# Early norms of the token parts, a refill of x inside the last pair, and first Down operands made ahead

## The chip, the cores and the metric

The kernel runs on one core of one Trainium2 chip, in one launch. The metric is the device time in microseconds, the median of the runs. Engines are named as in the profile: PE is TensorE, DVE VectorE, ACT ScalarE, POOL GpSimd, SP the engine that issues transfers.

## The reference

One step of a two-layer trunk in float32, for 1024 prompt frames and 32 sample frames, model width 1024. Layer 0 is retention and a ConvFFN, layer 1 is GLA (gated linear attention) and a ConvFFN.

```
h = rmsnorm(x, g)                      # per frame
q, k, v, g = split(h @ w_in)           # layer 0: 4 heads, q, k 256 wide, v, g 512
q, k = rotary(q, pos), rotary(k, pos)
S, o = chunked recurrence (q, k, v)    # S: 256 x 512 per head, decay per head
x = x + (silu(g) * groupnorm(o)) @ w_out
u = rmsnorm(x) @ w_up; c = 3-tap causal conv of u
x = x + (silu(gate) * val) @ w_down    # width 2816
```

All states and the last two rows of u are outputs too, and the frames end in a final RMSNorm.

## The kernel before

Frames stand in the columns and features in the 128 partitions: x is 8 tiles (kt) by 1056 columns, which are cut in four chunks of 264 (TH columns, 256 prompt and 8 sample frames each). A product of float32 accuracy is made of three matmuls: each operand is split in a rounded head and the rest (XA holds both for x, `whi` and `wlo` for a weight), and head by head, head by rest and rest by head are added in a PSUM bank. A weight tile is loaded to a `raw` tile by SP, ScalarE casts its head and VectorE subtracts.

Layer 0 starts in `ret_in`. Its first stage, the prelude, handles the four chunks one after the other. `normal(c)` squares x on ScalarE (L663), adds the squares on GpSimd for chunks 1 to 3 (L665), sums over partitions by matmuls with ones into `pn` (L671), makes 1/rms by a logarithm and an exponential on ScalarE and three operations on VectorE (the row, L673 and L166 to L168), and then `pair` scales x (L651, two tiles), casts the head (L654, ScalarE) and subtracts (L655, VectorE). `plain(j, c)` makes q or k of head 0 from it by 48 matmuls (L687 to L689, into `pj`); L690 copies them out. `sums(s)` adds chunks 2s and 2s+1 for the next stage.

That stage makes the gates of all heads and q, k of heads 1 to 3 with 14 units, two token halves and seven products each, a fast block product in which sums of blocks replace an eighth of the multiplications (`seven`, matmuls L351 to L356 into `pu`, 12 to a product). `put` adds products into a room of the buffer ARi (L718). What a product needs of the first feature half of an odd chunk is overwritten by sums, so that at the end of `ret_in` these parts are made again from x: the refill (L772 to L777), for each half one transfer, four multiplies, cast and subtraction.

Retention runs over four heads and nine steps (m) in each, eight for 128 prompt frames and one for the sample. The scores `pss` are masked (L492, `pm`), v is made into `psv` from weights wlo/wx, the outputs go to `po`, the state to `pu`, and the normalised output is `on` (L593).

`second(l)` then runs `Down` with w_ro (layer 0) or w_go (layer 1), the up projection with the convolution, `Down` with w_down, and for layer 0 the GLA. Down walks over column chunks; in each it goes through the weight tiles (kt), and for each through eight output columns (nt), each with a bank `pd` of its own. `load` fetches a tile's weight and its rows of the activation and splits both (XH, XB, hh, hl). When a column has its last tile, `evict` adds the bank to the residual (L1332, L1392). After the last chunk of layer 0's second Down the GLA's projections `pj` (L122) start.

Each engine runs its instructions in order, and the order is the program's, unless `order(a, b)` forces one; buffers come from pools with a fixed number of tiles, and from rooms cut by hand out of ARi. The order below is that of the built program.

## Time and profile before

| | |
|---|---|
| Median of 3 runs | 2955.16 us (2955.0 to 2959.51) |
| Profiled execution | 2953.43 us, span 2951.6 |
| TensorE busy | 2838.1 us (96%), 20658 matmuls |
| VectorE, ScalarE, GpSimd busy | 67%, 45%, 11% |
| Mean rate of transfers | 119 GB/s over the span |

The page divides the span in 40 slices of 74 us; TensorE's busy share is 0.4 in the first slice, 0.8 or more in all others, and the granted clock 0.7 in the first and 0.9 or more after it. A matmul record has a start and a modelled end, so that neighbours overlap; the step from start to start is what one costs. Times of the rows below are counted from the start of the span.

### The profile page before, as it was taken

How to read it: one execution, taken by the hardware profiler on the slowest of the kernel's cores; microseconds unless marked ns; L12 is line 12 of the kernel's file. 1: busy time of each engine (PE TensorE's matmuls, PEld its weight loads, DVE VectorE, ACT ScalarE, POOL GpSimd, SP SyncE). 2: the span in 40 equal slices, each digit the busy share in tenths (PEclk: the TensorE clock that was granted, in tenths of full speed). 3: DMA queues.
4: the chain of work that ended last, by engine and by line, in shares of the span. 5: the costliest groups of instructions: out<-in, count | busy, mean ns of one | idle time of the engine just before them, and what ended most of it. 6: DMA issues, size and time to landing. Idle time of an engine off the chain costs nothing.

```text
span 2951.6 us, 51990 instructions
## 1 busy us (share of the span) xinstructions
PE 2838.1 (96%) x20658; PEld 2732.8 (93%) x20658; DVE 1986.3 (67%) x3298; ACT 1325.7 (45%) x2375; POOL 335.7 (11%) x565
## 2 busy tenths in 40 slices
PE   4899989999899999999999999999998999999998
PEld 4899977878799999999999989999998999999998
DVE  6667546666578887777654577775488777786544
ACT  3332554343455444444543455554254444444443
POOL 1112000000002011111000032220011111110000
PEclk7999999999999999999999999999999999999999
DMA  3133343342576322222665511113652222227554
GB/s 118 37 95 117 110 151 101 94 127 82 176 250 191 112 73 80 80 74 82 218 198 172 185 43 47 47 40 130 202 173 74 86 80 73 87 69 239 179 162 142
DMA packets 206739, 353.83 MB, mean 120 GB/s; under 512 B 35712, under 2 KB 146432, under 8 KB 206496
## 3 DMA queue, kind: packets, MB, share of 16 engines
q1 hardware_dynamic: 205952, 349.93, 36.8%
q8 instruction: 161, 2.64, 0.4%
q14 instruction: 82, 0.67, 0.1%
q10 hardware_dynamic: 544, 0.59, 0.1%
HBM read 271.50 MB, written 78.95 MB: 119 GB/s over the span
## 4 chain that ended last, share of the span: by engine, by line
PE 85%; DVE 7%; DMA 3%; ACT 2%; issue 1%; POOL 1%; DVEq 0%; SPq 0%; ACTq 0%; POOLq 0%
PE pu L356 13%; PE pu L351 13%; PE pu L355 13%; PE pd L1171 7%; PE pd L1173 7%; PE pd L1172 7%; PE psv L245 2%; PE psv L244 2%; PE psv L246 2%; DMA raw<-w_ro 2%; PE pg L122 1%; PE pg L123 1%; PE pg L124 1%; PE pl L899 1%; PE pj L122 1%
## 5 line engine op out<-in xcount | busy, mean ns | idle before, releaser
L102 DVE TENSOR_TENSOR wlo<-raw,whi 128x1024 fp32r<-128x1024 f32 x226 | 283.7, 1257 | 259.4 <-ACT whi L102 250.3
L102 ACT CAST whi<-raw 128x1024 fp32r<-128x1024 f32 x226 | 236.4, 1049 | 313.2 <-PE pd L1172 219.5
L1171 PE MATMUL pd<-hh,whi 128*128 128x384 f32 (+1 forms) x880 | 284.9, 324 | 0.0
L1172 PE MATMUL pd<-hl,whi 128*128 128x384 f32 (+1 forms) x880 | 284.2, 323 | 0.1
L1173 PE MATMUL pd<-hh,wlo 128*128 128x384 f32 (+1 forms) x880 | 283.8, 323 | 0.0
L334 ACT COPY HR<-pu 128x264 f32<-128x264 f32 x264 | 99.0, 375 | 314.0 <-PE pu L356 311.5
L356 PE MATMUL pu<-XA,wgl 128*128 128x264 f32 x752 | 213.7, 284 | 0.7 <-DVE wgl L314 0.7
L355 PE MATMUL pu<-XA,wgh 128*128 128x264 f32 x752 | 212.9, 283 | 0.0
L351 PE MATMUL pu<-XA,wgh 128*128 128x264 f32 x752 | 212.8, 283 | 0.0
L1171 PE MATMUL pd<-XH,whi 128*128 128x264 f32 x576 | 164.2, 289 | 10.4 <-ACT XH L1146 7.6
L1172 PE MATMUL pd<-XH,whi 128*128 128x264 f32 x576 | 164.5, 287 | 2.7 <-DVE XH L1147 2.6
L1172 PEld LDWEIGHTS pd<-hl,whi 128*128 128x128 f32 x880 | 165.2, 188 | 0.9 <-DVE hl L1147 0.4
L1171 PEld LDWEIGHTS pd<-hh,whi 128*128 128x128 f32 x880 | 165.2, 188 | 0.4
L1173 PEld LDWEIGHTS pd<-hh,wlo 128*128 128x128 f32 x880 | 165.2, 188 | 0.1
L1239 DVE SCALAR_TENSOR_TENSOR AR<-AR,cw 128x1058 f32<-128x1058 f32 x88 | 116.0, 1318 | 72.1 <-ACT AR L1238 72.1
L1173 PE MATMUL pd<-XH,wlo 128*128 128x264 f32 x576 | 162.5, 287 | 0.7 <-DVE wlo L102 0.7
L314 DVE TENSOR_TENSOR wtl<-rv,wth 128x1024 fp32r<-128x1024 f32 x58 | 71.8, 1237 | 120.7 <-ACT wth L313 119.4
L1219 DVE TENSOR_TENSOR AR<-HR,pu 128x264 f32<-128x264 f32 (+2 forms) x440 | 144.7, 368 | 4.6 <-PE pu L356 4.6
L356 PEld LDWEIGHTS pu<-XA,wgl 128*128 128x128 f32 x752 | 141.2, 188 | 1.0 <-DVE wgl L314 1.0
L351 PEld LDWEIGHTS pu<-XA,wgh 128*128 128x128 f32 x752 | 141.3, 188 | 0.2 <-ACT wgh L313 0.2
L355 PEld LDWEIGHTS pu<-XA,wgh 128*128 128x128 f32 x752 | 141.2, 188 | 0.0
L351 PE MATMUL pu<-XA,wsh 128*128 128x264 f32 x464 | 132.0, 284 | 4.6 <-DVE ARi L718 2.5
(433 smaller groups left out, 9669.7 us busy)
## 6 DMA issues: line engine op xcount, KB each, us to landing
raw<-w_down SPq DMA_DIRECT2D x120, 512.0 KB, 3.6
raw<-w_ro SPq DMA_DIRECT2D x55, 512.0 KB, 4.4
rg<-w_up SPq DMA_DIRECT2D x44, 512.0 KB, 3.5
rv<-w_up SPq DMA_DIRECT2D x44, 512.0 KB, 3.5
scr_h<-AR SPq DMA_DIRECT2D x44, 512.0 KB, 2.7
HR<-scr_h SPq DMA_DIRECT2D x84, 192.0 KB, 3.7
raw<-w_go SPq DMA_DIRECT2D x23, 512.0 KB, 4.1
HR<-scr_or SPq DMA_DIRECT2D x64, 132.0 KB, 4.4
```

Of the source, the lines that this page charges most:

```text
L102: ins = S.copy(hi, raw), V.tensor_tensor(lo, raw, hi.bitcast(F32), op=ALU.subtract)
L122: PE.matmul(ps, hi[:, k], rh, start=kt == 0, stop=False)
L314: V.tensor_tensor(l_, src, h.bitcast(F32), op=ALU.subtract)
L334: S.copy(t, b)
L351: mm = PE.matmul(ps, wh[:, k], x[:, 0, kt], start=m in (1, 2, 4, 5) and kt == 0, stop=False, skip_group_check=True)
L355: PE.matmul(ps, wh[:, k], x[:, 1, kt], start=False, stop=False, skip_group_check=True)
L356: mm = PE.matmul(ps, wl[:, k], x[:, 0, kt], start=False, stop=kt == 3, skip_group_check=True)
L1171: PE.matmul(o, w[0][:, k], h[0][:, :n], start=i == 0, stop=False)
L1172: PE.matmul(o, w[0][:, k], h[1][:, :n], start=False, stop=False)
L1173: self.last_mm = PE.matmul(o, w[1][:, k], h[0][:, :n], start=False, stop=i == nk - 1)
L1219: V.tensor_tensor(u[:, d:d + n], t[:, o:o + n], b[:, o:o + n], op=op)
L1239: V.scalar_tensor_tensor(cj, uj[:, 1:T + 3], cw[:, nt, 1:2], cj, op0=ALU.mult, op1=ALU.add)
```

## The change

Five edits.

1. In `ret_in` the loads of chunk 0 stand first and its four squares ahead of the weight casts. Chunks 1 to 3 are squared with four tiles at a time, and the squares have a place of their own (`spare`), so that they need no tile of the weights' pool; chunk 0's x stands in `spare` too, and chunk 3 no longer waits for chunk 0's room. GpSimd adds 1056 and then 528 columns per chunk in place of 792 and 528, and two matmuls do instead of three. The row of chunk k+1 is placed within the k-th product. Each chunk's q and k are made one after the other. The second half of XC is allocated after `spare` is closed.
2. The rotations of head 0's q and k are placed between the products of the second token half, in units 1 to 4, with the room `ts` of ARi as their temporary. The second half starts after 8.5 products of the first instead of 7.3.
3. `refill` is called within the last unit, for each half as soon as its last product that needs the old values is issued. The first takes the room `ts`, the second `u`. The copies of the sample columns go to head 0, m = 2.
4. Both first Down objects are made before retention. In the last head's turn, `early` loads and splits weight tiles 0 and 1 and their rows for chunk 0.
5. In layer 0's second Down, last column chunk, the eight residual adds are issued first, and splits, squares and stores after the last of them.

```diff
+                if m == 4 and h + 1 == RH:
+                    d1s[0].early(0)
+                    d1s[0].early(1)
+                if m == 2 and h == 0:
+
+                    for j in range(4):
+                        for f in range(2):
+                            S.copy(xs[:, 4 * f:4 * f + 4, j * TS:j * TS + TS].rearrange("p k (c t) -> p k c t", c=4),
+                                   XP[:, :, f, j // 3, :, TH - 8:TH].rearrange("p c k t -> p k c t").bitcast(F32))
...
-        room = rooms(u=(AR, [8 * TH, 0, 4 * TH], 4 * TH), sn=ring(12 * TH, TH, 6, AR), ts=ring(18 * TH, 4 * TH, 1, AR))
...
+        room = rooms(u=(AR, [0, 8 * TH, 12 * TH], 4 * TH), sn=(AR, [o * TH for o in (4, 5, 6, 7, 16, 17)], TH),
+                     ts=ring(18 * TH, 4 * TH, 1, AR))
...
-        def normal(c):
-            per = 2 if c == 0 else 3
-            sq = []
+        def squares(c):
+            per = 2 if c == 0 else 4
+            sq = spare[:, (8 + c % 2 * 8) * TH:(16 + c % 2 * 8) * TH].rearrange("p (k t) -> p k t", k=KT)
             for kt in range(0, KT, per):
-                n = min(per, KT - kt)
-                t = w_tile(f"sq{uid()}").bitcast(F32)[:, :n * TH].rearrange("p (k t) -> p k t", k=n)
-                S.activation(t, xr[c][:, kt:kt + n], AF.Square)
-                if c and kt:
-                    G.tensor_tensor(sq[0][:, :n], sq[0][:, :n], t, op=ALU.add)
-                else:
-                    sq.append(t)
-            sq = [t[:, k] for t in sq for k in range(per)]
+                ins = S.activation(sq[:, kt:kt + per], xr[c][:, kt:kt + per], AF.Square)
+            n = KT
+            while c and n > 2:
+                n //= 2
+                G.tensor_tensor(sq[:, :n], sq[:, :n], sq[:, n:2 * n], op=ALU.add)
+            return sq, n, ins
+
+        def row(c, sq, n, after):
             ps = sm("pn")[:, :TH]
-            for i, t in enumerate(sq):
-                PE.matmul(ps, ones, t, start=i == 0, stop=i == len(sq) - 1)
-            t = w_tile(f"rm{uid()}").bitcast(F32)
-            V.tensor_scalar(t[:, :TH], ps, 1.0 / D, EPS, op0=ALU.mult, op1=ALU.add)
-            rsqrt(R[:, c * TH:c * TH + TH], t[:, TH:2 * TH], t[:, :TH])
+            for i in range(n):
+                mm = PE.matmul(ps, ones, sq[:, i], start=i == 0, stop=i == n - 1)
+                if after is not None:
+                    order(mm, after)
+            V.tensor_scalar(sq[:, 0], ps, 1.0 / D, EPS, op0=ALU.mult, op1=ALU.add)
+            rsqrt(R[:, c * TH:c * TH + TH], sq[:, 1], sq[:, 0])
+
+        def parts(c):
...
+        def refill(s):
+            c = 2 * s + 1
+            a = room("u" if s else "ts").rearrange("p (k t) -> p k t", k=4)
+            nc.sync.dma_start(a, io["xP"][:, c, 0:4])
+            for k in range(4):
+                V.scalar_tensor_tensor(a[:, k], a[:, k], gcol[:, 0, k:k + 1], R[:, c * TH:c * TH + TH],
+                                       op0=ALU.mult, op1=ALU.mult)
+            S.copy(XP[:, c, 0, 0], a)
+            V.tensor_tensor(XP[:, c, 0, 1], a, XP[:, c, 0, 0].bitcast(F32), op=ALU.subtract)
...
-        normal(0)
-        plain(0, 0)
-        normal(1)
-        plain(0, 1)
-        normal(2)
-        plain(0, 2)
-        plain(1, 0)
-        plain(1, 1)
-        sums(0)
-        for kt in range(0, KT, 4):
-            nc.sync.dma_start(xr[3][:, kt:kt + 4], io["xP"][:, 3, kt:kt + 4])
-        normal(3)
-        plain(0, 3)
-        plain(1, 2)
-        plain(1, 3)
-        sums(1)
-        weight_sums(0)
+        sq, n, ins = squares(0)
+        for j in range(2):
+            w0[j] = load_w(io["w_rqk"][0, j], None, (ins, None))
+        fetch(1, 4)
+        w0[2] = load_w(io["w_rqk"][0, 2])
+        row(0, sq, n, None)
+        fetch(2, 4)
+        fetch(3, 4)
+        w0[3] = load_w(io["w_rqk"][0, 3])
+        ones_ident()
+        cos = const("cos", [P, T], pl=rk)
+        sin = const("sin", [P, T], pl=rk)
+        gn = const("rgn", [P, 16], pl=rk)
+        parts(0)
         for c in range(4):
             for j in range(2):
-                ts = raw_tile(f"ts{uid()}")[:, :2 * TH].rearrange("p (j t) -> p j t", j=2)
-                rotate(qk0[c][:, j], ts, c, TH)
+                k = 2 * c + j
+                if k < 3:
+                    sq, n, _ = squares(k + 1)
+                mm = plain(j, c)
+                if k < 3:
+                    row(k + 1, sq, n, mm)
+            if c < 3:
+                parts(c + 1)
+            if c == 1:
+                sums(0)
+        first.close()
+        more(1, es.enter_context(pool("xd", side="right")).tile([P, 24 * TH], F32R, tag="XD", name="XD"))
+        weight_sums(0)
+        sums(1)
+        turns = [(c, j) for c in range(4) for j in range(2)]
         n = 7 * len(units)
-        seq = [(k, 0, k) for k in range(n)] + [(max(k + 3.5, 7.3 + 0.6 * k), 1, k) for k in range(n)]
+        seq = [(k, 0, k) for k in range(n)] + [(max(k + 3.5, 8.5 + 0.6 * k), 1, k) for k in range(n)]
...
-        for s in range(2):
-            c = 2 * s + 1
-            a = room("u").rearrange("p (k t) -> p k t", k=4)
-            nc.sync.dma_start(a, io["xP"][:, c, 0:4])
-            for k in range(4):
-                V.scalar_tensor_tensor(a[:, k], a[:, k], gcol[:, 0, k:k + 1], R[:, c * TH:c * TH + TH],
-                                       op0=ALU.mult, op1=ALU.mult)
-            S.copy(XP[:, c, 0, 0], a)
-            V.tensor_tensor(XP[:, c, 0, 1], a, XP[:, c, 0, 0].bitcast(F32), op=ALU.subtract)
+            if s == 1 and i in (2, 5) and f and turns:
+                c, j = turns.pop(0)
+                ts = room("ts")[:, :2 * TH].rearrange("p (j t) -> p j t", j=2)
+                rotate(qk0[c][:, j], ts, c, TH)
+            if f == len(units) - 1 and ORD[i] == 5:
+                refill(s)
...
+        held = []
         with pool("db") as dp:
             def evict(c, nt, a, ps, ss):
                 c0, n = CM[c]
                 V.tensor_tensor(a, a, ps, op=ALU.add)
-                split_x(2, a, nt, c0, n)
-                sumsq(ss, nt, a, n)
-                nc.sync.dma_start(scr_x[:, nt, c0:c0 + n], a)
+
+                def rest():
+                    split_x(2, a, nt, c0, n)
+                    sumsq(ss, nt, a, n)
+                    nc.sync.dma_start(scr_x[:, nt, c0:c0 + n], a)
+
+                held.append(rest)
+                while held and (c < 2 or nt == KT - 1):
+                    held.pop(0)()
...
+    d1s = [Down(16, lambda k: io["w_ro"][k], lambda k: scr_o[0][k], CQ, io["xT"], None, range(2, 5), 4),
+           Down(8, lambda k: io["w_go"][k], lambda k: scr_o[1][k], CQ, scr_x, None, range(2, 5), 4)]
```

ScalarE at the start of the program; `sq` and `sp` are squares, `whi` weight heads, XA the token parts. Before:

```order
L102 CAST whi_94<-raw_92 128x1024
...
L102 CAST whi_116<-raw_114 128x1024
L663 ACTIVATE sq_133<-ARi 128x528
...
L663 ACTIVATE sq_139<-ARi 128x528
L663 ACTIVATE sq_225<-ARi 128x792
L163 ACTIVATE rm_150<-rm_150 128x264
L164 ACTIVATE R<-rm_150 128x264
```

After:

```order
L667 ACTIVATE sp<-sp 128x528 x4
L102 CAST whi_108<-raw_106 128x1024
L102 CAST whi_114<-raw_112 128x1024
L164 ACTIVATE sp<-sp 128x264
L165 ACTIVATE R<-sp 128x264
L667 ACTIVATE sp<-ARi 128x1056 x2
L660 CAST XA<-sp 128x528
L102 CAST whi_122<-raw_120 128x1024
L660 CAST XA<-sp 128x528
L667 ACTIVATE sp<-ARi 128x1056 x2
L660 CAST XA<-sp 128x528 x2
L667 ACTIVATE sp<-ARi 128x1056
```

The squares of chunk 0 moved ahead of all weight casts, and those of chunks 1 and 2 between the casts of chunk 0's parts.

VectorE from the end of the products to the first mask of retention (`pm`); L718 and L730 are the adds of products, L774 and L755 the refill's multiplies, L777 and L758 its subtraction. Before:

```order
L774 SCALAR_TENSOR_TENSOR ARi<-ARi,gcol,R 128x264 x4
L102 TENSOR_TENSOR wlo_3956<-raw_3953,whi_3955 128x1024
L718 TENSOR_TENSOR ARi<-ARi,pu_3838 128x264
L718 TENSOR_TENSOR ARi<-ARi,pu_3778 128x264
L102 TENSOR_TENSOR wlo_4392<-raw_4389,whi_4391 128x1024
L777 TENSOR_TENSOR XA<-ARi,XA 128x1056
L718 TENSOR_TENSOR ARi<-ARi,pu_3838 128x264
L774 SCALAR_TENSOR_TENSOR ARi<-ARi,gcol,R 128x264 x4
L102 TENSOR_TENSOR wlo_4398<-raw_4395,whi_4397 128x1024
L777 TENSOR_TENSOR XA<-ARi,XA 128x1056
L492 TENSOR_TENSOR pm_3969<-pss_3966,rmask 128x128
```

After:

```order
L730 TENSOR_TENSOR ARi<-ARi,pu_3715 128x264
L755 SCALAR_TENSOR_TENSOR ARi<-ARi,gcol,R 128x264 x4
L730 TENSOR_TENSOR ARi<-ARi,pu_3823 128x264
L102 TENSOR_TENSOR wlo_3927<-raw_3924,whi_3926 128x1024
L758 TENSOR_TENSOR XA<-ARi,XA 128x1056
L730 TENSOR_TENSOR ARi<-ARi,pu_3763 128x264
L730 TENSOR_TENSOR ARi<-ARi,pu_3823 128x264
L102 TENSOR_TENSOR wlo_4371<-raw_4368,whi_4370 128x1024
L102 TENSOR_TENSOR wlo_4377<-raw_4374,whi_4376 128x1024
L488 TENSOR_TENSOR pm_3940<-pss_3937,rmask 128x128
```

The first refill's multiplies are no longer in this piece (they stand some 70 rows earlier), the second's moved from behind the last add of a product to ahead of the last three.

ScalarE at the end of retention; `on` is the normalised output of the last step, `vh` the head of v. Before:

```order
L264 CAST vh_7334<-psv_7309 128x512
L583 ACTIVATE ab_7353<-ab_7353 32x1
L206 ACT_TABLE_LOAD
L593 ACTIVATE on_7361<-po_7337,ab_7353 32x512
L102 CAST whi_7399<-raw_7397 128x1024
L102 CAST whi_7440<-raw_7438 128x1024
L1146 CAST XH_7393<-HR_7382 128x264 x2
L102 CAST XB_7394<-raw_7471 128x1024
```

After, in the sample step of the third head (`hs` are the rows made ahead, `whi` the weight of tile 0):

```order
L260 ACTIVATE kh_6447<-pk_6444,rcol 32x256
L1158 CAST hs_6944<-he_6942 128x264
L265 CAST vh_6485<-psv_6460 128x512
L516 CAST qh_6712<-qk_5953 128x256
L102 CAST whi_6949<-raw_6947 128x1024
L1158 CAST hs_6955<-he_6953 128x264
```

After, at the end of retention:

```order
L265 CAST vh_7335<-psv_7310 128x512
L588 ACTIVATE ab_7354<-ab_7354 32x1
L207 ACT_TABLE_LOAD
L598 ACTIVATE on_7362<-po_7338,ab_7354 32x512
L102 CAST XB_7395<-raw_7454 128x1024
L102 CAST XB_7395<-raw_7485 128x1024
L1175 CAST XH_7394<-HR_7383 128x264 x2
```

The casts of weight tile 0 moved some 70 rows ahead, and what follows the normalised output is now tile 2.

## Rows read from the trace of the kernel before

**Rows 1.** TensorE's waits: line, releaser, us in total, times, longest.

```profile
PE pj L687 <- ACT XA L654: 25.1, 4, 8.6
PE pn L671 <- ACT sq L663: 17.7, 1, 17.7
PE pd L1171 <- ACT XH L1146: 7.6, 1, 7.6
PE pj L122 <- DVE AR L1392: 3.1, 1, 3.1
```

**Rows 2.** Windows: length; PE, PEld, DVE, ACT, POOL busy; TensorE clock, DMA share, GB/s.

```profile
25.00:50.00 25.00, 12.00 (x59) 10.53 (x60) 18.29 (x29) 10.26 (x18) 7.72 (x6) 0.68 0.00 0
150.00:400.00 250.00, 250.00 (x2065) 250.00 (x2064) 155.18 (x219) 103.31 (x163) 37.24 (x24) 1.00 0.35 109
419.00:433.00 14.00, 9.35 (x22) 6.29 (x23) 8.94 (x16) 7.07 (x18) 0.86 (x5) 0.53 0.77 228
```

**Rows 3.** Timeline of ScalarE, 0 to 121 us: start, us, instruction, [idle before, releaser].

```profile
8.25 1.04 ACT L102 CAST whi<-raw 128x1024 fp32r<-128x1024 f32 x1 [6.23 <-DMA raw<-w_rqk]
...
120.96 0.38 ACT L690 COPY qk<-pj 128x264 f32<-128x264 f32 x1 [0.32 <-PE pj L689]
```

**Rows 4.** Timeline of TensorE, first 80 us.

```profile
17.68 6.83 PE L671 MATMUL pn<-sq,ones 128*128 128x264 f32 x16 [17.68 <-ACT sq L663]
...
29.28 0.81 PE L687 MATMUL pj<-XA,whi 128*128 128x264 f32 x2 [4.77 <-ACT XA L654]
...
77.72 0.42 PE L688 MATMUL pj<-XA,whi 128*128 128x264 f32 x1
77.94 0.42 PE L689 MATMUL pj<-XA,wlo 128*128 128x264 f32 x1
```

**Rows 5.** Lines of VectorE, 25 to 121 us: | busy us, mean ns | idle before.

```profile
L651 DVE SCALAR_TENSOR_TENSOR ARi<-ARi,gcol,R 128x264 f32<-128x264 f32 x32 | 19.8, 663 | 0.1
L655 DVE TENSOR_TENSOR XA<-ARi,XA 128x528 fp32r<-128x528 f32 x16 | 13.3, 829 | 1.0 <-ACT XA L654 0.9
L294 DVE TENSOR_TENSOR ARi<-ARi 128x1056 f32<-128x1056 f32 x8 | 10.0, 1249 | 0.1
L290 DVE TENSOR_TENSOR XC<-ARi,XC 128x1056 fp32r<-128x1056 f32 x6 | 7.4, 1247 | 1.9 <-ACT XC L289 1.9
...
L166 DVE TENSOR_TENSOR rm<-R 128x264 f32<-128x264 f32 x4 | 1.8, 452 | 2.2 <-ACT R L164 2.2
...
L314 DVE TENSOR_TENSOR wsl<-rg,wsh 128x1024 fp32r<-128x1024 f32 x1 | 1.2, 1224 | 0.2 <-ACT wsh L313 0.2
```

**Rows 6.** Timeline of VectorE, parts of chunks 0 and 2.

```profile
27.66 3.32 DVE L651 SCALAR_TENSOR_TENSOR ARi<-ARi,gcol,R 128x264 f32<-128x264 f32 x4
...
65.94 1.71 DVE L651 SCALAR_TENSOR_TENSOR ARi<-ARi,gcol,R 128x264 f32<-128x264 f32 x4
```

**Rows 7.** Timeline of GpSimd, the first sum of squares.

```profile
28.60 2.08 POOL L665 TENSOR_TENSOR sq<-sq,sq 128x792 f32<-128x792 f32 x1 [28.16 <-ACT sq L663]
```

**Rows 8.** Timeline of TensorE and VectorE, start of retention.

```profile
412.18 0.68 PE L489 MATMUL pss<-qk 128*128 128x128 f32 x4 [1.35 <-DVE ARi L718]
...
417.59 1.71 DVE L774 SCALAR_TENSOR_TENSOR ARi<-ARi,gcol,R 128x264 f32<-128x264 f32 x4 [5.55 <-DMA ARi<-xP]
...
428.85 0.79 PE L559 MATMUL po<-vh,ph 128*128 128x512 f32 x1 [0.68 <-ACT vh L543]
```

**Rows 9.** Timeline of VectorE, ScalarE and TensorE, end of retention.

```profile
775.21 1.22 DVE L568 SCALAR_TENSOR_TENSOR Sn<-S,pu 128x1024 f32<-128x1024 f32 x1
...
778.36 0.77 ACT L593 ACTIVATE on<-po,ab 32x512 f32<-32x512 f32 x1
...
783.86 0.59 PE L1172 MATMUL pd<-XH,whi 128*128 128x264 f32 x1 [0.48 <-DVE XH L1147]
...
791.53 0.28 PE L1171 MATMUL pd<-XH,XB 128*128 128x264 f32 x1
```

**Rows 10.** Timeline of VectorE, end of the second Down, layer 0.

```profile
1697.28 1.17 DVE L1392 TENSOR_TENSOR AR<-AR,pd 128x288 f32<-128x288 f32 x3
```

More of the change, by code (lines that the diff above doesn't have):

```diff
@@ L104, in load_w @@
             for a, b in zip(ins, after):
-                order(a, b)
+                if b is not None:
+                    order(a, b)
         return hi, lo
@@ L447, in retention @@
         xs = rp.tile([P, KT, P], F32R, tag="xs", name="xsr")
-        for j in range(4):
-            for f in range(2):
-                S.copy(xs[:, 4 * f:4 * f + 4, j * TS:j * TS + TS].rearrange("p k (c t) -> p k c t", c=4),
-                       XP[:, :, f, j // 3, :, TH - 8:TH].rearrange("p c k t -> p k c t").bitcast(F32))
         def value_weights(h):
@@ L623, in sm, with more, fetch @@
             return pp.tile([P, 512], F32, tag="ps", name=f"{name}{uid()}", bufs=8)
-        xr = [AR[:, c % 3 * 8 * TH:(c % 3 + 1) * 8 * TH].rearrange("p (k t) -> p k t", k=KT) for c in range(4)]
-        xc = XC.rearrange("p (o j k t) -> p o j k t", o=6, j=2, k=4)
-        X = [{1: XP[:, 2 * s, 0], 2: XP[:, 2 * s, 1], 5: XP[:, 2 * s + 1, 0], 3: XP[:, 2 * s + 1, 1],
-              6: xc[:, 3 * s], 7: xc[:, 3 * s + 1], 4: xc[:, 3 * s + 2]} for s in range(2)]
-        room = rooms(u=(AR, [8 * TH, 0, 4 * TH], 4 * TH), sn=ring(12 * TH, TH, 6, AR), ts=ring(18 * TH, 4 * TH, 1, AR))
-        w0 = {}
-        for kt in range(0, KT, 2):
-            nc.sync.dma_start(xr[0][:, kt:kt + 2], io["xP"][:, 0, kt:kt + 2])
-            if kt in (2, 6):
-                w0[kt // 6] = load_w(io["w_rqk"][0, kt // 6])
-        for c in (1, 2):
-            for kt in range(0, KT, 4):
-                nc.sync.dma_start(xr[c][:, kt:kt + 4], io["xP"][:, c, kt:kt + 4])
-            if c == 1:
-                for d in (2, 3):
-                    w0[d] = load_w(io["w_rqk"][0, d])
-        ones_ident()
-        cos = const("cos", [P, T], pl=rk)
-        sin = const("sin", [P, T], pl=rk)
-        gn = const("rgn", [P, 16], pl=rk)
+        first = ExitStack()
+        spare = first.enter_context(pool("sp", side="right")).tile([P, 24 * TH], F32, tag="sp", name="sp")
+        xr = [a[:, o * TH:(o + 8) * TH].rearrange("p (k t) -> p k t", k=KT)
+              for a, o in ((spare, 0), (AR, 0), (AR, 8), (AR, 16))]
+        X = [{1: XP[:, 2 * s, 0], 2: XP[:, 2 * s, 1], 5: XP[:, 2 * s + 1, 0], 3: XP[:, 2 * s + 1, 1]}
+             for s in range(2)]
+        def more(s, tile_):
+            X[s].update(zip((6, 7, 4), [tile_[:, o * 8 * TH:(o + 1) * 8 * TH].rearrange(
+                "p (j k t) -> p j k t", j=2, k=4) for o in range(3)]))
+        more(0, XC)
+        room = rooms(u=(AR, [0, 8 * TH, 12 * TH], 4 * TH), sn=(AR, [o * TH for o in (4, 5, 6, 7, 16, 17)], TH),
+                     ts=ring(18 * TH, 4 * TH, 1, AR))
+        def fetch(c, per):
+            for kt in range(0, KT, per):
+                nc.sync.dma_start(xr[c][:, kt:kt + per], io["xP"][:, c, kt:kt + per])
+        w0 = {}
+        fetch(0, 2)
         def pair(kt, c):
@@ L688, in plain @@
                     PE.matmul(ps, hi[:, k], l_, start=False, stop=False)
-                    PE.matmul(ps, lo[:, k], h, start=False, stop=kt == KT - 1)
+                    mm = PE.matmul(ps, lo[:, k], h, start=False, stop=kt == KT - 1)
                 S.copy(qk0[c][:, j, d], ps)
+                if d == 0:
+                    first = mm
+            return first
         def rotate(u, ts, c0, n):
@@ L735, in store @@
                                       u[:, d, :, o:o + n])
-        weight_sums, product = seven(X, wsrc, sm, lambda: room("sn"), begin, put, {})
-        normal(0)
-        plain(0, 0)
-        normal(1)
-        plain(0, 1)
-        normal(2)
-        plain(0, 2)
-        plain(1, 0)
-        plain(1, 1)
-        sums(0)
-        for kt in range(0, KT, 4):
-            nc.sync.dma_start(xr[3][:, kt:kt + 4], io["xP"][:, 3, kt:kt + 4])
-        normal(3)
-        plain(0, 3)
-        plain(1, 2)
@@ L1355, in done @@
                 return out[:4] + a + out[4:] + b
-            d1 = Down(ntile, lambda k: io[wo][k], lambda k: scr[k], CQ, scr_x if l else io["xT"], sm,
-                      range(2, 5), 4)
+            d1 = d1s[l]
+            d1.sm = sm
             ss, todo, xr = d1.run(droom, evict, norm, None, done)
```

2 lines of the change are left out of this document (1 added, 1 removed).

## The prediction

> **What bounds the kernel now.** I read three views in this order: the list of TensorE's waits, the windows, and then the timeline around each long wait. Over most of the run TensorE is simply full: from 150 to 400 us it is busy 250 of 250 us, 2065 matmuls of 264 columns, so 0.121 us each at the full clock of 2.4 GHz [rows 2]. Its idle time is about 113 us in all (span less busy time in the table above), and the four waits in [rows 1] hold 53.5 of it. Two sit in the first 121 us (25.1 on the ScalarE cast of the token parts, 17.7 until the first square), one is the first matmul of the first Down (7.6), one the first projection of the second layer (3.1). A fourth place is the start of retention: from 419 to 433 us TensorE is busy 9.35 of 14 us and its granted clock is 0.53 [rows 2]. A wait costs twice: after it the pitch is 0.22 us instead of 0.121, the lower level of 1.2 GHz [rows 4]. In the prelude the clock averages 0.68 from 25 to 50 us [rows 2].
>
> So each edit of this change is aimed at a place where TensorE waits; what counts is what is late next there.
>
> **Part 1, the prelude: norms early.** Before, ScalarE casts four weights (the first at 8.25, when its transfer had landed) and only then squares [rows 3]; TensorE's first norm matmul stands at 17.68, the 16 of them take 6.83, and 4.77 after their end the first projection runs [rows 4]. The chunks then follow one another: split, 48 matmuls, next norm, next split. The last copy of this stage is at 120.96 [rows 3].
>
> After, the four squares of chunk 0 stand first on ScalarE. The weight that landed by 8.25 was asked for behind half of chunk 0, so I put the norm matmuls at 7 (estimate; no earlier than 5, no later than the end of that cast, 9.3). They end at 13.8. The chain to the first projection was 4.77; one weight split now stands inside it, 1.2 [rows 5], which makes 19.8. VectorE starts on the parts at about 17.5.
>
> From there VectorE sets the pace, since the norms of chunks 1 to 3 are asked for a product earlier and no longer hang behind the chunk before. Its work up to the last part, from [rows 5]: parts 19.8 + 13.3; the row arithmetic of three chunks, four kinds at about 1.8 for four chunks, so 5.4; half of the operand sums (L294 5.0, L290 of XC and the two more of XA, half of some 10, 5.0); four weight splits 4.9. Together 53.4, so the last part is ready at 70.9, with half a microsecond of waits 71.4. Of the rest of the matmuls 78 remain (6 of the first product of the last chunk and three products of 24): 78 x 0.121 = 9.4, end at 80.8. TensorE alone: 192 matmuls at 0.22 and 192 at 0.121 from 19.8 make 85. I take 82 between the two: **39 us gained** against 120.96. Bounds: everything at the lower clock, 384 x 0.22 = 84.5 from 19.8, ends at 104, a gain of 17; no waits at all, 384 x 0.121 = 46.5, is out of VectorE's reach, so the upper end is VectorE's 53.4 without the contention below and 7 us sooner, a gain of 46.
>
> What goes with it: GpSimd's adds. While GpSimd adds squares (2.08 us for 792 columns [rows 7]), four of VectorE's multiplies take 3.32 instead of 1.71 [rows 6], so 1.61 of the 2.08 are lost to VectorE. The sum above has that in it, since the 19.8 and 13.3 were measured beside such adds. The adds grow from 792 + 528 to 1056 + 528 columns a chunk, some 0.7 us each for three chunks at the same rate, times 0.77: 1.6 us, inside my rounding.
> The Trainium skill, in "SBUF — State Buffer", section "Who interferes with whom", is harder: of a VectorE instruction with two inputs in SBUF and a GpSimd one that reads SBUF, the later one blocks fully until the first is done. The trace shows 1.61 lost of 2.08, not all; by the page the remaining quarter of some 12 us of adds would be lost too, and the sum below would come out about 3 us longer.
>
> The rotations of head 0's q and k leave the prelude and go between the products, eight pieces. There VectorE is busy 155 of 250 us and GpSimd 37 [rows 2]; each piece is two operations of 528 columns on VectorE (1.7 at L655's mean [rows 5]) and 528 columns on GpSimd (1.4 at the rate of [rows 7]), beside products of 12 matmuls, 1.46. Cover is ample; what could fail is the single temporary room (rival 4). The second token half starts 1.2 products later, which only reorders products. I charge **+1 us** (0 to 6) for new waits there.
>
> **Part 2, refill of x within the last pair.** Before, the second refill waits 5.55 us for its transfer, its four multiplies start at 417.59, and weight split, part and mask multiply queue behind it on VectorE [rows 8]. TensorE loses 14 - 9.35 = 4.65 us of idle time from 419 to 433 and, at clock 0.53, 0.47 x 9.35 = 4.4 more [rows 2]: 9 us. The products end at 412.18 - 1.35 = 410.8 [rows 8]. After, the transfer is asked for behind the stores of the last unit but one, some 8 us before the end of the products (counted in products of 1.46). VectorE may wait there about 2 us for it, with a bank-freeing add and one weight split queued behind; TensorE's last product can be held by some tenths. Then cast, part, two more adds, two weight splits (2.4) and only then the mask multiply: I count it at 7 to 8 us after the end of the products, and the first output matmul at 12 to 13, against 428.85 - 410.8 = 18 before [rows 8]. So about 5 us less idle time and perhaps half of the clock's 4.4: **7 us**. Bounds: 2 (the transfer is as late as before) and 10 (all of it). The copies of the sample columns, eight small casts, move into the first head, where ScalarE is not waited for: nothing, or up to 1.7 us if the first cast of v stands behind them.
>
> **Part 3, the first operands of Down made ahead.** Before, TensorE waits 7.6 us for the first tile [rows 1], and the third weight tile's first matmul stands at 791.53 [rows 9]. After, tiles 0 and 1 are ready. TensorE still waits twice in the first pass over eight output columns, since two banks are read late: VectorE's state update ends at 775.21 + 1.22 = 776.43, ScalarE's normalised output at 778.36 + 0.77 = 779.13 [rows 9]. The banks stand at the second and the sixth column. So tile 0 ends at 779.1 + 9 x 0.121 = 780.2, tile 1 at 783.1. Tile 2 needs its part of the loaded rows, ready at about 784 as tile 0's was before (783.86 [rows 9]). 791.5 - 784 = 7.5; for the lower clock after those waits I take one off: **6.5 us**, bounds 3 (both tiles at 0.22: 48 x 0.1 = 4.8 more) and 8. The operands made ahead are two casts on ScalarE and two subtractions on VectorE for each tile, none over 1.2 [rows 5], in the sample steps of heads 2 and 3; up to 0.7 us, in the minus one.
>
> **Part 4, second Down of layer 0, last chunk: adds first.** The next projection waited 3.1 us [rows 1] for the bank of the sixth column, whose add stood behind splits and squares at 1697.28 [rows 10]. After, the eight adds stand together and the bank is free when TensorE comes. The splits and squares behind them feed a norm that TensorE reaches 8 us later. **2.5 us** (0 to 3.1).
>
> **Sum.** The profiled execution took 2953.43 (span 2951.6 and 1.83 around it), 1.7 below the median. 2953.4 - 39 + 1 - 7 - 6.5 - 2.5 = 2899.4; with the median's offset 2901. I say 2900.
>
> **Rivals.**
> 1. The prelude stays at the lower clock: waits for parts keep coming every 6 to 10 us, as they did when the clock was 0.68 [rows 2]. Gain 17 instead of 39: 2921. For it: the first two chunks will have such waits. Against it: from the third chunk on TensorE has a backlog of products that need no new part. The Trainium skill, in "TensorE: Matmul & The Clock Gate", section "HAM oscillation — how this bites in real kernels", tells of a kernel that fell back to the lower clock at each wait for data; the pitch of 0.22 in [rows 4] agrees.
> 2. The squares aren't early: chunk 0 itself lands late, and the norm matmuls start near 17 as before. Then part 1 loses 10: 2910. Against it, the cast at 8.25 [rows 3].
> 3. Both boundaries only trade waits: the refill's transfer still holds VectorE, and the banks of the last step hold the first Down. Parts 2 and 3 give 2 + 3 instead of 13.5: 2908, or 2914 if nothing at all.
> 4. Slower: the temporary room. Eight rotations and twelve stores pass through one room, each holding VectorE until GpSimd's two adds are done; with the 28 half-units of the loop that is a chance for TensorE to run dry 20 times. At 3 us a time (VectorE's pair and GpSimd's pair exposed) it costs 60, and the kernel is slower by 5. It decides from 2.7 us a time. Against it: before, the twelve stores used that same room and TensorE had no idle time from 150 to 400 [rows 2].
>
> **Chances.** The forecast 0.70 (own range 2889 to 2908), rival 1 0.12, rival 2 0.05, rival 3 0.08, rival 4 0.03, something of no effect 0.02. The range 2886 to 2924 reaches from all upper bounds at once (-46 - 10 - 8 - 3 makes 2886) to rival 1 with a little of rival 3. What a measurement can tell from no change is about 0.2%, 6 us: faster 0.94, same 0.03, slower 0.03.
>
> **What would show it.** The last copy of the first projections near 82 instead of 121, and the first norm matmul near 7. A windows row near clock 1.0 from 60 us on; if it is near 0.6 there, rival 1 holds. At the retention start, mask multiply 7 to 8 us after the last product, with a VectorE wait of 1 to 3 us for the xP transfer. At Down, two waits of 1 to 2.5 us (on the state update and on the normalised output) in place of 7.6. No wait on L122 of the second layer. New waits on ARi between 90 and 370 us would be rival 4.

## The result, and the profile after

The changed kernel takes 2905.98 us (median of 4 runs, 2905.13 to 2910.6) beside 2955.08 for the kernel before on the same chip: a ratio of 0.9834, 95% interval 0.9817 to 0.9851, or 49 us less. The forecast was 2900. The profiled execution has a span of 2904.9 us, 46.6 less than before. Divided at the same five instructions in both traces, the span gives the table below. Three of the five of before are in [rows 3, 8, 9]; the other two are here, the last matmul of retention's state and the first GLA projection, before and then after:

```profile
L557 PE MATMUL pu<-vh,kh x8: 387/390/397, 511.4 to 774.5; 128*128 128x512 f32 x8
1697.77 0.44 PE L122 MATMUL pj<-XA,whi 128*128 128x384 f32 x1 [3.06 <-DVE AR L1392]
```
```profile
L562 PE MATMUL pu<-vh,kh x8: 387/394/398, 476.8 to 740.6; 128*128 128x512 f32 x8
1653.06 0.35 PE L123 MATMUL pj<-XA,whi 128*128 128x384 f32 x1
```

| Stage, us | before | after | difference | forecast |
|---|---|---|---|---|
| start to the last q, k copy | 121.0 | 79.7 | -41.3 | -39 |
| to the first scores (products) | 291.2 | 302.0 | +10.7 | +1 |
| to the last state matmul (retention) | 362.3 | 359.0 | -3.3 | -7 |
| to the third weight tile of Down | 17.0 | 8.7 | -8.3 | -6.5 |
| to the first GLA projection | 906.2 | 903.7 | -2.5 | -2.5 |
| to the end | 1253.8 | 1251.9 | -1.9 | 0 |

The list of TensorE's waits of the kernel after (us in total, times, longest) answers to [rows 1]:

```profile
PE pu L352 <- DVE ARi L730: 9.4, 5, 3.1
PE pj L697 <- DVE XA L661: 7.1, 4, 3.2
...
PE pj L696 <- ACT XA L660: 5.2, 2, 4.5
PE pn L677 <- ACT sp L667: 5.0, 1, 5.0
...
PE pss L485 <- DVE pm L488: 2.7, 1, 2.7
```

Of the four in [rows 1], the 25.1 us on the cast of the parts have become 5.2 and the 17.7 until the first square 5.0; the 7.6 at Down and the 3.1 on the first GLA projection are gone. At the head stands a wait that before made 2.5 us in two places: products on the adds of other products (L730, before L718). The wait on the subtraction of the parts (7.1) was 6.0 before.

The windows after, against [rows 2], with the prelude in four of them:

```profile
0.00:25.00 25.00, 12.24 (x40) 9.96 (x40) 14.68 (x17) 13.02 (x17) 7.01 (x8) 0.80 0.92 345
25.00:50.00 25.00, 20.49 (x136) 19.13 (x137) 20.34 (x33) 12.27 (x22) 4.91 (x3) 0.93 0.07 22
50.00:75.00 25.00, 24.99 (x206) 24.78 (x205) 25.00 (x38) 13.61 (x23) 0.00 (x0) 1.00 0.01 2
75.00:100.00 25.00, 24.17 (x194) 23.48 (x194) 20.94 (x27) 13.21 (x20) 5.37 (x6) 1.00 0.24 67
110.00:360.00 250.00, 241.21 (x1946) 240.37 (x1945) 157.87 (x225) 96.17 (x153) 47.91 (x34) 0.98 0.34 104
```

The clock is 1.00 from 50 to 100 us, so that rival 1 did not come true. But in the products TensorE, busy 250 of 250 us before, now loses 8.8 us in a stretch as long.

The timeline of TensorE at the start, the last part on VectorE and the last copy of the prelude on ScalarE, against [rows 4] and [rows 3]:

```profile
4.95 6.62 PE L677 MATMUL pn<-sp,ones 128*128 128x264 f32 x16 [4.95 <-ACT sp L667]
16.09 0.81 PE L696 MATMUL pj<-XA,whi 128*128 128x264 f32 x2 [4.53 <-ACT XA L660]
20.07 0.59 PE L697 MATMUL pj<-XA,whi 128*128 128x264 f32 x1 [3.17 <-DVE XA L661]
...
68.72 0.70 DVE L661 TENSOR_TENSOR XA<-ARi,XA 128x528 fp32r<-128x528 f32 x1
...
79.69 0.37 ACT L699 COPY qk<-pj 128x264 f32<-128x264 f32 x1
```

The norm starts at 4.95, the earlier bound of the forecast, not at 7. From its end to the first projection it is 4.53 us (forecast: 4.77 plus 1.2 for a split), and the last part is ready at 69.42, where 70.9 was forecast.

**Where the products lose.** VectorE and then TensorE around 167 us, and GpSimd just before:

```profile
163.85 1.65 POOL L708 TENSOR_TENSOR ARi<-ARi 128x528 f32<-128x528 f32 x1 [2.72 <-ACT ARi L335]
165.46 1.32 POOL L709 TENSOR_TENSOR ARi<-ARi 128x528 f32<-128x528 f32 x1
```
```profile
166.82 0.71 DVE L706 TENSOR_TENSOR ARi<-qk,sin 128x528 f32<-128x528 f32 x1 [2.51 <-POOL ARi L709]
...
168.19 1.22 DVE L315 TENSOR_TENSOR wtl<-rv,wth 128x1024 fp32r<-128x1024 f32 x1
169.32 1.10 DVE L730 TENSOR_TENSOR ARi<-ARi,pu 128x264 f32<-128x264 f32 x3
```
```profile
169.80 0.39 PE L352 MATMUL pu<-XA,wsh 128*128 128x264 f32 x1 [3.07 <-DVE ARi L730]
...
171.16 0.42 PE L356 MATMUL pu<-XA,wsh 128*128 128x264 f32 x1
...
174.24 0.39 PE L352 MATMUL pu<-XA,wgh 128*128 128x264 f32 x1
174.46 0.29 PE L356 MATMUL pu<-XA,wgh 128*128 128x264 f32 x1
```

A rotation of head 0 stands ahead of a weight split and of three adds that free banks, and waits 2.51 us for GpSimd's rotation of the unit that is being stored, which uses the same room. TensorE waits 3.07 us; then the 14 matmuls from 171.16 to 174.24 take 0.22 us each, the level of 1.2 GHz, 1.4 us more than at 0.121. The same happens at 194.93 (2.96). At 280.29 (2.12) what stands in the way is the first refill, on VectorE:

```profile
275.75 0.69 DVE L319 TENSOR_TENSOR rv<-rv 128x512 f32<-128x512 f32 x1 [5.82 <-DMA rv<-w_rg]
277.06 1.71 DVE L755 SCALAR_TENSOR_TENSOR ARi<-ARi,gcol,R 128x264 f32<-128x264 f32 x4 [0.62 <-DMA ARi<-xP]
278.68 1.22 DVE L315 TENSOR_TENSOR wtl<-rv,wth 128x1024 fp32r<-128x1024 f32 x1
279.82 1.10 DVE L730 TENSOR_TENSOR ARi<-ARi,pu 128x264 f32<-128x264 f32 x3
```

It is called within the last unit, near 365 us, and runs at 277. So the build moves an operation ahead of where it is called when its room and its operands allow. I had taken the order to be the program's, though the pieces of the order printed ahead of the prediction showed the multiplies some 70 rows earlier.

**The two boundaries**, against [rows 8] and [rows 9]. VectorE and TensorE at the start of retention, TensorE at the first Down:

```profile
377.96 1.71 DVE L755 SCALAR_TENSOR_TENSOR ARi<-ARi,gcol,R 128x264 f32<-128x264 f32 x4 [2.35 <-DMA ARi<-xP]
...
391.56 0.29 DVE L488 TENSOR_TENSOR pm<-pss,rmask 128x128 f32<-128x128 f32 x1 [2.55 <-DMA rmask<-rmask]
```
```profile
381.64 0.61 PE L485 MATMUL pss<-qk 128*128 128x128 f32 x4
...
396.25 0.52 PE L564 MATMUL po<-vh,ph 128*128 128x512 f32 x1
```
```profile
742.55 0.39 PE L1200 MATMUL pd<-hs,whi 128*128 128x264 f32 x1 [1.20 <-DVE Sn L573]
745.25 0.39 PE L1200 MATMUL pd<-hs,whi 128*128 128x264 f32 x1 [0.99 <-ACT on L598]
749.32 0.28 PE L1200 MATMUL pd<-XH,XB 128*128 128x264 f32 x1
```

At Down both waits are those forecast. At retention the wait on the xP transfer (2.35) is as forecast too, but the mask multiply is 9.9 us behind the first scores, not 7 to 8 (421.61 - 412.18 = 9.4 before), held by a transfer that the prediction did not have on its list: the masks' own.

### The profile page after: what moved, and what is told of

It reads as the page before. It is cut to its first block, busy times and chain, and to the rows that moved or that the text cites. A ratio compares the mean times of both kernels' runs of the same rounds, so it can differ in the third digit from the quotient of the medians.

```text
span 2904.9 us, 51957 instructions
## 1 busy us (share of the span) xinstructions
PE 2830.5 (97%) x20652; PEld 2726.3 (94%) x20652; DVE 1984.3 (68%) x3298; ACT 1323.4 (46%) x2372; POOL 339.2 (12%) x565
## 4 chain that ended last, share of the span: by engine, by line
PE 78%; DVE 6%; DMA 2%; ACT 2%; issue 1%; POOL 1%; SPq 0%; DVEq 0%; ACTq 0%; POOLq 0%
PE pu L357 11%; PE pu L352 11%; PE pu L356 11%; PE pd L1200 7%; PE pd L1202 7%; PE pd L1201 7%; PE psv L246 2%; PE psv L245 2%; PE psv L247 2%; DMA raw<-w_ro 2%; PE pg L123 1%; PE pg L124 1%; PE pg L125 1%; PE pl L928 1%; PE pv L245 1%
## 5 line engine op out<-in xcount | busy, mean ns | idle before, releaser
L1200 PE MATMUL pd<-XH,whi 128*128 128x264 f32 x560 | 158.6, 287 | 2.6 <-ACT whi L102 2.5
L1201 PE MATMUL pd<-XH,whi 128*128 128x264 f32 x560 | 158.4, 285 | 1.6 <-DVE XH L1176 1.6
L1202 PE MATMUL pd<-XH,wlo 128*128 128x264 f32 x560 | 156.6, 285 | 0.6 <-DVE wlo L102 0.5
```

What stands on the lines that cost most here:

```text
L1200: PE.matmul(o, w[0][:, k], h[0][:, :n], start=i == 0, stop=False)
L1201: PE.matmul(o, w[0][:, k], h[1][:, :n], start=False, stop=False)
L1202: self.last_mm = PE.matmul(o, w[1][:, k], h[0][:, :n], start=False, stop=i == nk - 1)
```

## The experiments

All start from the kernel after; ratios are to the kernel before.

**What makes the products wait.** First the room: another temporary for the rotations.

```diff
-                ts = room("ts")[:, :2 * TH].rearrange("p (j t) -> p j t", j=2)
+                ts = raw_tile(f"ts{uid()}")[:, :2 * TH].rearrange("p (j t) -> p j t", j=2)
```

> The changed kernel with one edit: the eight rotations of head 0 between the products take a raw weight tile as their temporary instead of the room ts that the stores' rotations use. Theory (one room, two users): the waits of 3.07 and 2.96 us on ARi near 170 and 195 us go, with them the lower clock behind each (window 168 to 174 at 0.75), in all 8 to 10 us, about 2897; the 2.12 us wait near 280 stays. Rival (VectorE and GpSimd simply have too much to do there, or collide on SBUF): the waits stay within 1 us, time within 2 us of 2906.

2906.61 us, 0.9836 (0.9822 to 0.9851): no gain. The waits stay, 2.52, 3.86 and 2.20 us near 167, 191 and 277. VectorE now waits for a weight transfer instead. On SP's queue stores stand ahead of two weight loads, and the second load is asked for only when GpSimd's add of a rotation is done (159.11 + 1.78 = 160.89), since the rotation's temporary is now one of the three raw weight tiles:

```profile
141.32 17.34 SPq L739 DMA_DIRECT2D scr_q<-ARi  x4
158.76 0.43 SPq L309 DMA_DIRECT2D rg<-w_rqk  x1
160.92 0.35 SPq L309 DMA_DIRECT2D rv<-w_rqk  x1
```
```profile
159.11 1.78 POOL L709 TENSOR_TENSOR qk<-qk,ts 128x264 f32<-128x264 f32 x1
```
```profile
164.47 0.82 DVE L319 TENSOR_TENSOR rv<-rv 128x512 f32<-128x512 f32 x1 [2.47 <-DMA rv<-w_rqk]
```

So a second temporary alone, at least one taken from the weights, does not help: in the change VectorE waits for the room, here for a transfer, and both wait for GpSimd, which has two rotations in one q, k unit. That this is the cause is a guess so far. Next, both refills at the end again.

```diff
-            a = room("u" if s else "ts").rearrange("p (k t) -> p k t", k=4)
+            a = room("u").rearrange("p (k t) -> p k t", k=4)
...
-            if f == len(units) - 1 and ORD[i] == 5:
-                refill(s)
+        for s in range(2):
+            refill(s)
```

> The changed kernel with the refill undone: both refills after the last unit, in the room u, as before. Theory: the first refill in the room ts is what holds VectorE near 277 us (its four multiplies stand ahead of a weight split), so the 2.12 us wait near 280 goes, some 4 us with its clock; at the start of retention 7 to 9 us come back (first output matmul 18 us after the products instead of 14.6, lower clock behind it). Net 3 to 6 us slower than 2906. Rival (the refill as changed is worth its full 4.7 us and the wait near 280 is from the gate weights' late transfer): that wait stays, net 5 to 9 us slower.

2904.77 us, 0.983: the wait near 280 goes, as the theory had it, but neither price holds, the undoing costs nothing. The products take 300.1 us; at retention the wait on the mask is 4.3 us instead of 2.7. In this kernel VectorE waits for the same `rv` transfer (5.05 us), but its bank-freeing adds follow the split at 276.19 instead of 279.82.

Rotations called only in gate units, which have no rotation of their own:

```diff
-            if s == 1 and i in (2, 5) and f and turns:
+            if s == 1 and i in (2, 5) and f >= 8 and turns:
```

> The changed kernel with the eight rotations of head 0 moved from units 1 to 4 into units 8 to 11, which are gate units whose stores use no GpSimd; the room stays ts. New theory (in the q, k units the rotation's adds on GpSimd push back the store's adds, and with them SP's stores, the next weight transfer that stands behind them on SP, and VectorE's split of it): the two waits of 3 us near 170 and 195 us go, and the wait near 280 too, since the first refill now stands behind the last rotation; products stage 291 to 295 us instead of 302, time 2896 to 2900. Rival (the products are slower for another reason, the later second half or the clock): the waits move to the gate units, stage over 299, time within 2 us of 2906.

2903.52 us, 0.9824 (0.9809 to 0.9839). The waits near 170, 195 and 280 are gone, but 3.59 and 3.88 us stand at 269.71 and 295.86; at the second VectorE waits for the transfer of the first refill (5.26 us). With the refills at the end as well:

> As the one with late rotations, and the refills at the end as before the change. If the refill is worth what was forecast (7 us), this is 5 to 8 us slower than late rotations alone; if the refill only moves its waits (the mask multiply stands behind the loaded masks in either), within 2 us of it.

2901.47 us, 0.9818; the products take 293.1 us, with one long wait left (3.60 at 269.59). There all eight rotations run between 257 and 287 us, though they are called over some 80. Calling one a unit (`i == 5 and f >= 5`) was to space them:

> The rotations stand one to a unit, in the eight gate units 5 to 12, and both refills at the end. Theory: a gate unit has no rotation adds of its own on GpSimd, so that one rotation a unit is done long before the next asks for the room; the waits of 3.6 and 0.8 us that two a unit left at 269 and 293 us go, with some 2 us at the lower clock behind them. Products stage 288 to 290 instead of 293.1, time 2896 to 2899 against 2901.5. Rival: a rotation anywhere costs about 0.5 us of TensorE, whatever the distance (eight of them 4 us); then the stage stays at 292 to 294 and the time at 2900 to 2903.

2901.26 us, 0.9817: the rival's figure, but not its reason. (The expectation is wrong on one point: units 5 to 7 are q, k units, not gates.) The calls are 20 us apart; VectorE's last five run so, as soon as the last q, k store has freed the room:

```profile
259.99 0.71 DVE L706 TENSOR_TENSOR ARi<-qk,sin 128x528 f32<-128x528 f32 x1 [0.88 <-POOL ARi L709]
...
269.52 0.71 DVE L706 TENSOR_TENSOR ARi<-qk,sin 128x528 f32<-128x528 f32 x1 [1.56 <-POOL qk L709]
```

The first waits for GpSimd's adds for that store, each of the others for those of the rotation before it, and TensorE waits 3.26 us at 271.76. In another kernel the rotations stand ahead of all products, as before the change:

> The change with one part undone: head 0's rotations stand ahead of all products, as before the change (temporary in room ts); the refill stays in place. Theory: the waits near 170 and 195 us go and the one near 280 stays (5 us with its clock); the eight rotations are 8 x 3 us of VectorE and GpSimd at the start, beside the first projections' last operands, and hold the first blocks: 5 to 12 us between 75 and 120 us. Time 2903 to 2911. Rival: the start is free since products can run ahead of them; then only the 8 us of the waits near 170 and 195 go, and the time is 2896 to 2900.

2905.1 us, 0.9828 (0.9815 to 0.9842), as the theory had it: waits of 0.84, 3.02 and 1.91 us between 88 and 113, none near 170 and 195, 2.10 at 275.

Then the two kernels in which the order is forced: each rotation behind the product it is called after, and in the first of the two the refills' multiplies behind the last product that uses the old values (the second `order` in the diff).

```diff
+            ins = V.tensor_tensor(ts, u, sb, op=ALU.mult)
+            if after is not None:
+                order(ins, after)
...
+                order(ins, after)
...
+            mm = product(f, s, i, None)
...
+            if s == 1 and i in (2, 5) and f >= 8 and turns:
...
+                rotate(qk0[c][:, j], ts, c, TH, mm)
...
+                refill(s, mm)
```

> Head 0's rotations two to a unit in the gate units 8 to 11, each held back in VectorE's order behind the product it is called after; the refills where the change puts them, their multiplies held back behind the product that uses the old values last. Theory: the long waits of the products stage (9.4 us on ARi in all, and 2 us at the lower clock behind each) come from rotations and multiplies that are issued early, as soon as a room is free, and so stand ahead of a weight split or of one another. With both held back the waits near 170, 195, 270 and 280 us go: stage 289 to 293 instead of 302, and the refills in place give back the 1.5 us at the start of retention; span 2893 to 2897, time 2895 to 2899. Rival: VectorE's added work there costs TensorE in itself, wherever it stands; then waits of 3 us appear at other places, the stage stays at 293 to 299 and the time at 2901 to 2905.

2894.18 us (2892.66 to 2895.64), 0.9791 (0.9777 to 0.9804): the theory, a little better than its range. All waits in the products but one are gone, and they take 288.0 us, 14 less than after and 3 less than before. TensorE's waits from 75 to 405 us in this kernel, all of them:

```profile
365.29 0.39 PE L352 MATMUL pu<-XA,wsh 128*128 128x264 f32 x1 [2.15 <-DVE ARi L732]
373.21 0.49 PE L245 MATMUL psv<-wx,XA 128*128 128x512 f32 x1 [1.06 <-ACT wx L102]
376.08 0.79 PE L485 MATMUL pss<-qk 128*128 128x128 f32 x2 [2.37 <-DVE pm L488]
377.21 0.80 PE L246 MATMUL psv<-wx,XA 128*128 128x512 f32 x1 [0.34 <-DVE wx L102]
```

VectorE shows the rotations spread up to 325 us, and the first refill at its product instead of 74 us ahead of it. The one wait left belongs to the second refill, whose transfer is late:

```profile
325.25 0.70 DVE L706 TENSOR_TENSOR ARi<-qk,sin 128x528 f32<-128x528 f32 x1
...
350.40 1.70 DVE L757 SCALAR_TENSOR_TENSOR ARi<-ARi,gcol,R 128x264 f32<-128x264 f32 x4
...
360.74 1.70 DVE L757 SCALAR_TENSOR_TENSOR ARi<-ARi,gcol,R 128x264 f32<-128x264 f32 x4 [1.48 <-DMA ARi<-xP]
```

The second keeps the forced rotations and has the refills at the end.

> As the kernel with everything held back, but both refills at the end of the stage in room u, as before the change. It tells what the refill in place is worth once it no longer stands in the way. Theory: the stage is as short (289 to 292) or 1 us shorter, and the wait of 5 us on the mask multiply at the start of retention is there again, against 2 to 3 us with the refills in place: 2 to 4 us slower than that kernel, 2897 to 2902. Rival: the transfer is asked for hardly earlier in place, so both are within 1 us of each other.

2892.78 us (2891.2 to 2894.11), 0.9787 (0.9774 to 0.9801), the lowest median, and the rival's answer: the two cannot be told apart. From the last copy of the prelude to the last state matmul it is 646.3 us with the refills in place and 647.0 with them at the end. Both intervals lie wholly below that of the change. This kernel differs from the one of 2901.47 us (late rotations, refills at the end) by the forced order alone, and their intervals (0.9774 to 0.9801, 0.9803 to 0.9832) do not meet: with the rotations in the same units, the forced order took the products from 293.1 to 286.6 us.

**The start of retention: masks loaded early**, into the room of the cosines, so that 2.66 us of wait on the mask go.

```diff
+            if f == 9 and s == 1 and i == 0:
+                nc.sync.dma_start(cos[:, :RH * P].rearrange("p (h t) -> p h t", h=RH), io["rmask"])
...
```

> The changed kernel with one edit: retention's mask and decay columns are loaded in the tenth unit into the tile that held the cosines, instead of after the products. Theory (the first mask multiply waits for that transfer, 2.55 us, asked for behind the last stores): the 2.66 us wait of the second score matmul goes to under 0.5, 3 to 4 us faster than 2906 with the clock. Rival (the refill's chain on VectorE and ScalarE is late anyway): the wait passes to the weight casts wx behind it, under 1.5 us.

2907.96 us (2907.57 to 2908.46): no gain. The wait on the mask is gone, and others stand there: 1.54 us on `kl`, 1.50 on ScalarE's cast `wx`, 0.76 and 0.72 behind them. Several chains end within about a microsecond of each other here.

**The prelude: no sums of squares on GpSimd**; the eight square tiles of a chunk go to TensorE.

```diff
-            while c and n > 2:
+            while False:
```

> The changed kernel with GpSimd's adds of the squares left out for chunks 1 to 3: TensorE sums all eight square tiles with ones, 8 matmuls instead of 2 each. Theory (GpSimd's adds stop VectorE's multiplies almost for their whole length: 4.92 us for four instead of 1.71): the twelve multiplies beside adds take 0.43 each, the parts of chunk 0 end near 23 instead of 28.1; TensorE's norm rows cost 5 us more each where it has nothing else at first, so the prelude ends within 4 us of 79.7 either way. Rival (the multiplies are slow by themselves, from the first read of loaded rows): they stay at 0.8 to 1.2 us and the prelude ends 8 to 12 us later.

2905.81 us: no net change, but the contention shows. VectorE's first four multiplies, in this kernel and then in the kernel after:

```profile
14.49 1.71 DVE L657 SCALAR_TENSOR_TENSOR sp<-sp,gcol,R 128x264 f32<-128x264 f32 x4
```
```profile
14.48 4.92 DVE L657 SCALAR_TENSOR_TENSOR sp<-sp,gcol,R 128x264 f32<-128x264 f32 x4
```
```profile
15.04 4.07 POOL L671 TENSOR_TENSOR sp<-sp 128x1056 f32<-128x1056 f32 x2 [14.60 <-ACT sp L667]
```

Of GpSimd's 4.07 us VectorE loses 3.21. Taken one by one, in narrow windows of the timeline, the second and third multiply and the first add of the kernel after:

```profile
14.89 0.49 DVE L657 SCALAR_TENSOR_TENSOR sp<-sp,gcol,R 128x264 f32<-128x264 f32 x1
15.29 2.66 DVE L657 SCALAR_TENSOR_TENSOR sp<-sp,gcol,R 128x264 f32<-128x264 f32 x1
```
```profile
15.04 2.62 POOL L671 TENSOR_TENSOR sp<-sp 128x1056 f32<-128x1056 f32 x1 [14.60 <-ACT sp L667]
```

The multiply that was under way when the add began keeps its 0.49 us; the one that starts during the add ends at 17.95, 0.29 behind the add's end (17.66). So it is held for the whole rest of the add, and what VectorE does not lose is the multiply already under way.

The prelude ends at 76.5, beside 79.7 in the kernel after and 77.8 to 79.6 in the other kernels with this prelude, so leaving the adds out is worth 1.3 to 3.2 us there. The products take 304.0 us, 2 more than after; a wait of 1.50 us on ARi at 86.63, which the kernel after does not have, is part of that. The rest is not settled.

**First Down without tiles made ahead** (the two `early` calls taken out).

> The changed kernel without the two weight tiles and rows made ahead for the first Down. Theory: the wait of 7.6 us on the cast of the rows is back, the third tile's first matmul comes 16 to 17.5 us after the last state matmul instead of 9; 7 to 9 us slower than 2906. Rival (the transfers of the first Down are the limit anyway): the 8 us are given back later in the Down, under 3 us slower.

2913.45 us (2910.32 to 2919.81). The wait on the first tile is back (7.64 us, [rows 1] had 7.6) and the stage takes 17.6 us instead of 8.7; the next one is 2 us shorter. The edit is worth about 7.

**Second Down without adds first** (`while held:`).

> The changed kernel with the residual adds of layer 0's second Down not held together: the wait of 3.1 us on the sixth bank is back at the first projection of the second layer, and 2 to 3 us are lost up to there; the GLA behind it stays as it is, so 2 to 3 us slower than 2906. Rival (the chain of norm and gates behind it sets the end of that stretch): under 1 us.

2912.27 us (2909.64 to 2913.74). The wait of 3.06 us is back; the stretch from Down's third tile to the projection is 909.4 instead of 903.7. The wait explains 3 of the 5.7; before the change the stretch was 906.2. Most of the rest lies where the edit does nothing: in the first 100 us of the stretch, in the first Down, TensorE waits 6.2 us beside 3.8 in the kernel after, most of it for the weights' casts. So the traces show 3 us for the adds first; that the medians differ by 6 is open beyond that.

## Why the prediction was right, and which of its steps were wrong

- **Prelude, -39 forecast, -41.3 measured.** Right in size, and in the mechanism as far as the traces tell. VectorE started on the parts at 14.48 instead of 17.5 and was through at 69.42, 1.5 us slower than the 53.4 of the sum. From 50 to 75 us it is busy 25.00 of 25 us, but TensorE is busy 24.99 at clock 1.00 as well (its waits for parts, 12.3 us, all end before that), so that the two paces came out nearly equal, and which of them sets the end is not shown. The forecast for TensorE alone (85) was too late: some 40 of the 384 matmuls ran at 0.22, not 192. The share lost to GpSimd's adds carried over: 3.21 of 4.07 is 79%, beside 77% before. But the prediction's reading, that not all is lost, was wrong: before too, the multiply that starts within an add, at 28.88, ends at 30.98, 0.30 behind the add of [rows 7] (28.60 + 2.08). The Trainium skill, "SBUF — State Buffer", section "Who interferes with whom", speaks of an exclusive lock; these rows agree with it.
- **Products, +1 forecast (0 to 6), +10.7 measured. This step failed**, at "Cover is ample; what could fail is the single temporary room". A busy share of 155 in 250 us on VectorE and 37 on GpSimd says that there is room, not that it lies where the operation stands. What failed was the place in the order: rotations in units where GpSimd turns two more, and a refill 90 us before its call, each ahead of a weight split and bank-freeing adds. Waits of 0.76, 0.64, 3.07, 2.96, 2.12 and 0.56 us make 10.1, and 14 matmuls at the lower clock behind each of the three long ones 3 x 1.4; before, the stage had 4.6 us of such waits (0.75, 1.69, 0.80, 1.35). The rotations in gate units and the order forced took the stage to 288.0, under before. Forced rotations within the q, k units were not tried. Rival 4's sign (waits on ARi between 90 and 370 us) came, and in two of them its price of 3 us; but four times and not 20. That the room alone makes them was not borne out, since another temporary left them in place.
- **Refill, -7 forecast (2 to 10): -0.7 with the order forced, nothing as it was built. This step failed too**, at the mask multiply "7 to 8 us after the end of the products". The transfer does come earlier (wait 2.35 instead of 5.55), but the masks' own transfer, which the sum left out, holds the mask multiply 9.9 us behind the first scores. From the last copy to the last state matmul the change takes 660.9 us, with the refills at the end 659.6. This is the half of rival 3 that held. Of the stage's -3.3 most is there with the refills at the end (359.5, and 360.4 with the rotations forced, against 362.3); its cause was not tried. The copies of the sample columns are no clear candidate: called in the third step of the first head, they run at 392.75, still ahead of the first cast of v, where the prediction put a price of up to 1.7 us. That cast waits 0.23 us for TensorE behind them, so no price is seen.
- **Down, -6.5 forecast, -8.3 measured**, with both waits at the named places; 2 of it are given back later.
- **Adds first, -2.5 forecast, -2.5 in the trace**; the wait that comes back without them is 3.06.
- **The sum.** The terms that came out better (2.3 + 1.8 + 1.9 at the end, where nothing was changed) made up for part of the two that came out worse (9.7 + 3.7): 2906 instead of 2900. That it came so close is in part luck: had nothing come out better, it would have been 6 us further off.

## What to carry to other kernels

Work that is moved under a full TensorE needs a place as well as cover: look at what stands behind it in the engine's queue (a split, an add that frees a bank), and who else holds the unit that it waits for. If the build may pull an operation ahead when its buffer is free, a later call alone may change little (eight rotations called over 80 us ran within 30); force the order. A buffer that comes free later may do the same, but was not tried. And before taking away the wait that ends last, list the others that end within a microsecond of it.

## What the runs showed of the hardware

- Behind each of the three long waits in the products after (3.07, 2.96 and 2.12 us) stand 14 matmuls at 0.22 us instead of 0.121, 1.4 us more. The Trainium skill, "TensorE: Matmul & The Clock Gate", section "HAM oscillation — how this bites in real kernels", has such a fall behind waits for data; these rows agree. But behind the wait of 2.15 us in the kernel with everything forced the clock stays at 1.00 (365 to 371 us), as it does behind those of 0.76 and 0.64 after, and behind the 2.52 us at 166.82 in the kernel with the raw temporary the next 160 matmuls run at 0.121. So the length of the wait alone does not decide it, and "a wait costs twice" in the prediction holds for some waits only.
- A VectorE multiply of two tensors that starts while GpSimd adds is held until that add is done: 2.66 us instead of 0.49, ending 0.29 us behind it (0.30 in the trace before).
- Over longer stretches too like waits do not always bring the same clock: in the 100 us from the first GLA projection the kernel with everything forced was granted 0.95, the one with refills at the end 0.98, at like waits. A single trace can't settle 2 us.
